# Projections in a deep Trainium2 kernel: one token tile after the other, or both in turns on each chunk of weights

## The chip, the core and the metric

The kernel runs on one core of one Trainium2 chip. The core has five engines that run side by side: TensorE (PE in the profile; PEld is its loading of the stationary operand), VectorE (DVE), ScalarE (ACT), GpSimd (POOL) and SyncE (SP), which here issues the DMA loads of all weights. Each engine takes its instructions in the order of its own queue, and an instruction that waits holds up everything behind it on that engine. The metric is the time of one execution in microseconds.

## What is computed

256 tokens of 1024 features go through nine sublayers, all in float32: two blocks of (FFN, mixer, FFN), where the first mixer is HGRN2 and the second is forgetting attention ("fox"), and a third block (FFN, token mixer, FFN) that is modulated by a vector c. The FFNs hold most of the products:

```python
def swiglu(h, w_in, w_out):                      # w_in 1024 x 5632, w_out 2816 x 1024
    gate, up = jnp.split(h @ w_in, 2, axis=-1)
    return (jax.nn.silu(gate) * up) @ w_out
...
proj = h @ w_in                                  # fox: q, k, v, g (1024 columns each), z_f
...
mod = (jax.nn.silu(c) @ w_ada[l] + b_ada[l]).reshape(b, N_SUB, 3, D_MODEL)   # third block
u = rms_norm(h, norm_pre[l, i]) * (1.0 + scale) + shift
h = h + resid_w * gate * rms_norm(fn(u), norm_post[l, i])
```

## The kernel before

**Products.** The tokens are two token tiles of 128 (t = 0 and 1). A sublayer's normalized input is transposed (L233) and split into a high part `uh` (a cast on ACT) and a rest `ul` (a subtraction on DVE), both by `split` (L166, L167). The activations are the stationary operand, and the weights stream through. Weights are split in the same way into `H` (ACT) and `L` (DVE), and each product is three passes (`mm3`): H by uh (L208), L by uh (L209), H by ul (L210).

**Weights.** They come in chunks of two k-tiles (2 x 128 rows) of 512 columns, 512 KB each. SP loads a chunk into one of five `raw` buffers (L177); the splits of a chunk free its buffer for the chunk five places on; `H` and `L` have six chunks each. A projection of 512 columns takes four chunks and eight k-tiles. `project` goes over them for one token tile: 8 k-tiles x 3 passes = 24 matmuls into one PSUM bank `acc` (five banks in that pool). The first projection to ask for a chunk loads it, the second token tile's 24 matmuls use the same tiles again.

**FFN** (`ffn`, L478). Its 2816 columns are cut into `SLICES`: five of 512 and one, the third, of 256. For each slice TensorE runs gate of t 0, the transposes of the slice before, gate of t 1, up of t 0, up of t 1. `gate` is a Silu on ACT, `up` a product on DVE. `out_stream` then adds up the product with `w_out` (22 k-tiles). A sublayer's first slice goes through `first_pair` (L387), which puts the second token tile's transposes behind the first products of t 0.

**Modulation beside it.** The third block's modulation is computed in jobs of 512 columns (`ada`, L844), spread over the sublayers 3, 5, 6, 7 and 8 (counted from 0; 4, 4, 4, 4 and 2 jobs). A job loads four chunks of `w_ada` through the same five `raw` buffers (L849) and a row of `b_ada`, and adds them up with two DVE operations a chunk (L851); its end is a split and two matmuls (L858). `side()` runs one step of a job; an FFN calls it after each projection of one token tile from the second slice on, four times a slice, and on in the out projection.

**Mixers.** `group(g)` makes two projections of both tiles by `pair` (L416) or, in the token mixer, by `values` and `both`. The small products of attention are tasks that `weave` puts between the pieces of projections by a planner's costs (`PACING`). In hgrn these are the decays (L612), scores (L636 to L645) and outputs (L660); in fox a head's scores (L783, L784), transposes (L793) and values (L802 to L804), with DVE's minimum (L787), ACT's exponential (L789), a DVE copy (L795) and a DVE product by the gate (L815) between them.

**Order.** TensorE's order is that in which the code is traced. Other engines' queues are ordered by a scheduler, in advance.

Of the kernel before, what the change touches and what calls it, by code (L numbers as in the profile page):

```python
"""Two pre-norm blocks of two layers (HGRN2 and forgetting attention as mixers), then a
modulated block with stick-breaking and differential attention, on 256 tokens.

Layout: the residual stream stays in SBUF as two tiles of 128 tokens. Every projection has
the activations (transposed, [feature, token]) as the stationary operand and streams the
weights. Both operands are split exactly into a part of float32r's 12 significant bits and
a rest, and hi*hi + hi*lo + lo*hi are summed in PSUM, so each product costs three
single-rate passes at float32's accuracy. The mixers' small products are plain float32.
"""
# [13 lines left out]
ALU = mybir.AluOpType  # L23
# [5 lines left out]
P = 128  # L29
# [4 lines left out]
CK = 2      # k-tiles of 512 columns in a chunk of weights  # L34
# how many tasks of a mixer are under way, the time between their starts and what else their chains take (see weave)
# [3 lines left out]
# (first column, columns) of the hidden slices of a feed-forward layer  # L39
SLICES = ((0, 512), (512, 512), (1024, 256), (1280, 512), (1792, 512), (2304, 512))  # L40

# columns of the array of constants
C_U = 0                 # [128, 9, 128] partial-sum columns: level 128 (first tile), 64..1, 128 (second tile)
C_LM = C_U + 9 * 128    # [128, 7, 64] which scores a level supplies
C_FOXM = C_LM + 7 * 64  # [128, 256] zeros | causal mask
C_SEL = C_FOXM + 256    # [128, 16] -1 in rows h and 32 + h of column h
C_DIST = C_SEL + 16     # [128, 384] -|t - s|, chunk-causal
C_STR = C_DIST + 384    # [128, 384] s < t
C_SUF = C_STR + 384     # [128, 128] -(j > s)
C_WIDE = C_SUF + 128    # [128, 128] the diagonal and the pairs of levels 64 and 32  # L50
# [3 lines left out]
def constants():  # L54
    """Arrays that depend on shapes alone."""
# [12 lines left out]
    c[:, C_FOXM + P:C_FOXM + 2 * P] = np.where(t <= s, 0.0, NEG)   # rows are queries here  # L68
# [3 lines left out]
    for k, (q0, k0) in enumerate(((0, 0), (P, 0), (P, P))):  # L72
        qp, kp = s + q0, t + k0                                    # rows are queries
        c[:, C_DIST + k * P:C_DIST + (k + 1) * P] = np.where(kp // 64 <= qp // 64, -np.abs(qp - kp), -1e34)
    for k, (k0, q0) in enumerate(((0, 0), (0, P), (P, P))):
        c[:, C_STR + k * P:C_STR + (k + 1) * P] = (s + k0) < (t + q0)   # rows are keys
# [5 lines left out]
class Program:  # L82
    """Traces the computation. The order of the tensor engine's instructions is that of this code (the
    other engines are left to the scheduler), so code that feeds it from slower chains is written as
    tasks (generators, see weave) that are woven into the streams of projections."""

    def __init__(self, tc, p, es):
# [36 lines left out]
        self.jobs = []      # generators that are run beside the projections, a step at a time  # L124

    def side(self):
        """A step of the jobs."""
# [41 lines left out]
    def loadw(self, views, shape, spare=False):  # L169
        """One chunk of weights, split: the views side by side in its last dimension. Returns (hi, lo) of its  # L170
        two halves (k-tiles, or columns of one k-tile). Spare chunks take tiles that stand idle at the ends
        of sublayers."""
# [243 lines left out]
    def pair(self, W1, W2, evac1, evac2, after1, after2, transposes=None):  # L416
# [4 lines left out]
        else:  # L421
            for t in range(NT):
                yield from self.project(t, W1, evac1)
# [801 lines left out]
```

## Time and profile before

| | |
|---|---|
| median of 3 runs | 1718.08 us (1717.99 to 1723.05) |
| span of the profiled execution | 1713.2 us (first to last instruction) |
| outside that span, against the median | 4.9 us |
| TensorE busy | 1667.1 us, 97% |
| VectorE busy | 1144.1 us, 67% |
| ScalarE busy | 911.8 us, 53% |
| GpSimd busy | 212.5 us, 12% |
| DMA | 328.45 MB, 192 GB/s on the mean |

One execution was profiled; its own device time was not listed apart, so the median of the three stands beside its span. Busy time of TensorE counts a matmul to its modelled end, which overlaps the next; the pitch from one start to the next is what a matmul costs. "Idle" in brackets is what an engine waited just before an instruction, with the engine and line that it waited for. PEclk is the granted clock, 1.00 at 2.4 GHz and near 0.5 at 1.2 GHz.

### The profile page before, as it was taken

Reading aid. Unit: us, or ns where it says so; the run is one execution under the profiler, and the core shown is the slowest. Engines: PE = TensorE matmul, PEld = TensorE weight load, DVE = VectorE, ACT = ScalarE, POOL = GpSimd, SP = SyncE. Lnnn points to the kernel's source line nnn. Section 1 sums busy time; section 2 is a strip of 40 time slices with the busy share of each in tenths; the row PEclk is TensorE's granted clock in tenths of the full one; section 3 lists DMA queues with packets and bytes.
Section 4 is the critical chain, followed back from the end, with each engine's and each line's share of the span. In section 5 each row is a group of like instructions: output and inputs, shape, how many; then the busy total and the mean of one; then the engine's idle time right before and its main releaser. Section 6 shows DMA issues by size and latency. Waiting matters only on the chain. (4 is left out here: it accounts for less than half of the span.)

```text
span 1713.2 us, 23351 instructions
## 1 busy us (share of the span) xinstructions
PE 1667.1 (97%) x8136; PEld 1386.2 (81%) x8136; DVE 1144.1 (67%) x2003; ACT 911.8 (53%) x1884; POOL 212.5 (12%) x275
## 2 busy tenths in 40 slices
PE   7999999999999999999999999999999999999998
PEld 5888888788888888888888878878887678778886
DVE  5555587776655677656566767578756678877663
ACT  5545466555544545546665544445545558564452
POOL 2000034330000010003120000110003321120000
PEclk9999999999999999999999999999999999999999
DMA  9555543325656588755345776568764456746652
GB/s 305 177 191 197 183 150 99 99 77 178 212 183 202 172 262 276 238 170 176 122 150 161 242 250 239 167 208 296 256 225 146 159 178 201 248 157 219 226 196 75
DMA packets 176886, 328.45 MB, mean 192 GB/s; under 512 B 12656, under 2 KB 65904, under 8 KB 176768
## 3 DMA queue, kind: packets, MB, share of 16 engines
q1 hardware_dynamic: 173328, 318.29, 56.4%
q0 software_dynamic: 3152, 8.15, 1.7%
q8 instruction: 64, 1.05, 0.2%
q14 instruction: 54, 0.44, 0.1%
q10 hardware_dynamic: 288, 0.52, 0.1%
HBM read 325.86 MB, written 1.05 MB: 191 GB/s over the span
## 5 line engine op out<-in xcount | busy, mean ns | idle before, releaser
L167 DVE TENSOR_TENSOR L<-raw,H 128x512 fp32r<-128x512 f32 (+1 forms) x1092 | 694.9, 681 | 221.6 <-ACT H L166 214.1
L166 ACT CAST H<-raw 128x512 fp32r<-128x512 f32 (+1 forms) x1092 | 599.4, 600 | 426.7 <-PE acc L210 301.8
L208 PE MATMUL acc<-H,uh 128*128 128x512 f32 (+1 forms) x1552 | 600.0, 387 | 1.3 <-ACT uh L166 1.3
L209 PE MATMUL acc<-L,uh 128*128 128x512 f32 (+1 forms) x1552 | 588.5, 379 | 5.9 <-DVE L L167 5.7
L210 PE MATMUL acc<-H,ul 128*128 128x512 f32 (+1 forms) x1552 | 587.0, 378 | 0.5 <-DVE ul L167 0.5
L209 PEld LDWEIGHTS acc<-L,uh 128*128 128x128 f32 x1552 | 294.1, 190 | 61.1 <-DVE L L167 12.0
L210 PEld LDWEIGHTS acc<-H,ul 128*128 128x128 f32 x1552 | 293.5, 189 | 55.5 <-DVE ul L167 1.4
L208 PEld LDWEIGHTS acc<-H,uh 128*128 128x128 f32 x1552 | 294.0, 189 | 52.7 <-ACT uh L166 1.9
L208 PE MATMUL acc<-H,w 128*128 128x512 f32 x536 | 209.8, 391 | 0.0
L209 PE MATMUL acc<-L,w 128*128 128x512 f32 x536 | 208.6, 389 | 0.0
L210 PE MATMUL acc<-H,q 128*128 128x512 f32 x512 | 199.4, 389 | 0.0
L851 DVE SCALAR_TENSOR_TENSOR ad<-raw,cs,ad 128x512 f32<-128x512 f32 x144 | 109.5, 761 | 93.5 <-DMA raw<-in_w_ada 78.6
L209 PEld LDWEIGHTS acc<-L,w 128*128 128x128 f32 x536 | 100.7, 188 | 20.6
L208 PEld LDWEIGHTS acc<-H,w 128*128 128x128 f32 x536 | 100.6, 188 | 20.5
L210 PEld LDWEIGHTS acc<-H,q 128*128 128x128 f32 x512 | 96.1, 188 | 20.1
L276 POOL TENSOR_SCALAR r<-s 128x1 f32<-128x1 f32 x24 | 15.9, 664 | 724.3 <-ACT o L259 482.3
L493 ACT ACTIVATE o<-acc 128x512 f32<-128x512 f32 (+1 forms) x72 | 40.4, 561 | 75.2 <-PE acc L210 75.1
L167 DVE TENSOR_TENSOR q<-T,w 128x512 fp32r<-128x512 f32 (+1 forms) x72 | 43.6, 639 | 45.6 <-ACT w L166 45.6
L233 PE MATMUL T<-ident,o 128*128 128x128 f32 x408 | 55.6, 276 | 14.5 <-DVE o L265 9.7
L498 DVE TENSOR_TENSOR o<-o,acc 128x512 f32<-128x512 f32 (+1 forms) x72 | 45.9, 637 | 34.9 <-PE acc L210 34.7
L233 PEld LDWEIGHTS T<-ident,o 128*128 128x128 f32 x408 | 47.7, 142 | 23.6 <-DVE o L265 9.7
L845 POOL MEMSET ad<- 128x512 f32 x18 | 9.5, 529 | 394.4 <-DVE ad L167 368.7
(244 smaller groups left out, 1440.6 us busy)
## 6 DMA issues: line engine op xcount, KB each, us to landing
raw<-in_ffn_w_in SPq DMA_DIRECT2D x160, 512.0 KB, 4.7
raw<-in_ffn_w_out SPq DMA_DIRECT2D x88, 512.0 KB, 4.2
raw<-in_w_ada SPq DMA_DIRECT2D x72, 512.0 KB, 5.2
raw<-in_ffn_w_down SPq DMA_DIRECT2D x44, 512.0 KB, 4.3
raw<-in_ffn_w_gate SPq DMA_DIRECT2D x40, 512.0 KB, 4.5
raw<-in_ffn_w_up SPq DMA_DIRECT2D x40, 512.0 KB, 4.5
raw<-in_hg_w_in SPq DMA_DIRECT2D x64, 256.0 KB, 3.2
raw<-in_fox_w_in SPq DMA_DIRECT2D x64, 256.0 KB, 3.6
```

The lines of the kernel that those rows point to most:

```text
L166: self.nc.scalar.copy(hi, src)
L167: self.nc.vector.tensor_sub(lo, src, hi.bitcast(F32))
L208: mm(out, xh, H, start=first, stop=False)
L209: mm(out, xh, L, start=False, stop=False)
L210: mm(out, xl, H, start=False, stop=last)
L233: self.nc.tensor.transpose(T[:, j, :], src[:, (k0 + j) * P:(k0 + j + 1) * P], self.ident)
L276: self.nc.gpsimd.tensor_scalar(r, s2[:, 0:1], s2[:, 1:2], EPS, op0=ALU.add, op1=ALU.add)
L493: self.last_silu = nc.scalar.activation(s[:, :n], A[:, :n], AF.Silu)
L498: nc.vector.tensor_tensor(s[:, :n], s[:, :n], A[:, :n], op=ALU.mult)
L845: nc.gpsimd.memset(a, 0.0)
L851: nc.vector.scalar_tensor_tensor(a, raw[:, k, :], self.cs[:, k0 + k:k0 + k + 1], a, op0=ALU.mult, op1=ALU.add)
```

## The change

A new generator, `project_both`, goes through a projection's four chunks and lets both token tiles use each chunk before the next. `pair` (in hgrn and fox), the token mixer's projections and the FFN's gates and ups use it; `first_pair` stays as it is. In the FFN's 256-column slice, gate's and up's columns are loaded side by side and make one product of 512 columns. `side()` still runs four steps in a slice of 512 columns, after every 8 of its 16 pieces of a projection, but two in that of 256. Comments are removed as well, which shifts line numbers: L166, L167 and L208 to L210 stay, L233 is L240 after, L265 is L272, L851 is L866, L793 is L808, L802 is L817.

```diff
+    def project_both(self, W, evac):
+        states = [{} for _ in range(NT)]
+        for k0 in range(0, 8, CK):
+            for t in range(NT):
+                yield from self.project(t, W, evac, k0, k0 + CK, states[t])
...
-            for t in range(NT):
-                yield from self.project(t, W1, evac1)
+            yield from self.project_both(W1, evac1)
             yield from after1
-            for t in range(NT):
-                yield from self.project(t, W2, evac2)
+            yield from self.project_both(W2, evac2)
         yield from after2
...
-            if c0:
-                self.side()
+
+        def run_both(W, evac, between=None):
+            for n, _ in enumerate(self.project_both(W, evac)):
+                if n == 7 and between is not None:
+                    transposes(*between)
+                if n % 8 == 7:
+                    self.side()
...
+            def gate_up(t, A):
+                gate(t, A)
+                up(t, A)
...
+            elif n == 256:
+                run_both(self.load_in([wgc, wuc], n), gate_up, before)
             else:
-                run(self.project(0, Wg, gate))
-                transposes(*before)
-                run(self.project(1, Wg, gate))
-                for t in range(NT):
-                    run(self.project(t, Wu, up))
+                run_both(self.load_in([wgc], n), gate, before)
+                run_both(self.load_in([wuc], n), up)
```

**TensorE in the second slice of the first FFN**, before: the end of `up` of the first token tile (bank acc_453) and the start of the second's (bank acc_511), which takes its weights from the start again.

```order
L208 MATMUL acc_453<-H_498,uh0_111 128x512
L209 MATMUL acc_453<-L_499,uh0_111 128x512
L210 MATMUL acc_453<-H_498,ul0_113 128x512
L208 MATMUL acc_511<-H_456,uh1_112 128x512
L209 MATMUL acc_511<-L_457,uh1_112 128x512
L210 MATMUL acc_511<-H_456,ul1_114 128x512
```

And the same projection now, from its second chunk (H_477) to the third (H_497):

```order
L208 MATMUL acc_453<-H_477,uh0_111 128x512
L209 MATMUL acc_453<-L_478,uh0_111 128x512
L210 MATMUL acc_453<-H_477,ul0_113 128x512
L208 MATMUL acc_468<-H_477,uh1_112 128x512
L209 MATMUL acc_468<-L_478,uh1_112 128x512
L210 MATMUL acc_468<-H_477,ul1_114 128x512
L208 MATMUL acc_468<-H_477,uh1_112 128x512
L209 MATMUL acc_468<-L_478,uh1_112 128x512
L210 MATMUL acc_468<-H_477,ul1_114 128x512
L208 MATMUL acc_453<-H_497,uh0_111 128x512
```

Each chunk now has 12 matmuls in a row, six for each tile; before, a chunk's two uses stood 24 matmuls apart, and the four chunks of a projection were first asked for within its first 24.

**VectorE at the start of sublayer 3**, the first with jobs, before. `o` are the halves of the normalized second token tile, `ul_114` the rest of its transposed halves, without which TensorE's passes L210 of that tile can't run, and `ad` is the sum of the first job.

```order
L265 SCALAR_TENSOR_TENSOR o_5229<-X_108,rs_5236,mod 128x512
L265 SCALAR_TENSOR_TENSOR o_5230<-X_108,rs_5236,mod 128x512
L167 TENSOR_TENSOR ul_114<-T,uh_112 128x512 x2
L167 TENSOR_TENSOR L<-raw,H 128x512 x8
L851 SCALAR_TENSOR_TENSOR ad<-raw,cs,ad 128x512
```

And the same place now:

```order
L272 SCALAR_TENSOR_TENSOR o_5073<-X_108,rs_5080,mod 128x512
L272 SCALAR_TENSOR_TENSOR o_5074<-X_108,rs_5080,mod 128x512
L866 SCALAR_TENSOR_TENSOR ad<-raw,cs,ad 128x512
L167 TENSOR_TENSOR ul_114<-T,uh_112 128x512 x2
L866 SCALAR_TENSOR_TENSOR ad<-raw,cs,ad 128x512
L167 TENSOR_TENSOR L<-raw,H 128x512 x8
```

The first step of a job has moved from behind eight weight splits to ahead of `ul_114`. On SP its load stands two chunks earlier too, in the eleventh place of the sublayer instead of the thirteenth. The starts of sublayers 5, 6, 7 and 8 show the same.

**TensorE at the end of fox**, before: the last head's values (L802 to L804), out products `acc<-H,o`, and the last transposes (L233).

```order
L802 MATMUL T<-q_8276,w_8417 128x64
L803 MATMUL T<-q_8276,w_8417 128x64
L804 MATMUL T<-q_8357,w_8417 128x64
L208 MATMUL acc<-H,o_6998 128x512
...
L210 MATMUL acc<-H,o_6999 128x512
L233 MATMUL T<-ident,w_8477 128x128 x2
L233 MATMUL T<-ident,w_8482 128x128 x2
```

And now, from the last out product that stands between the heads: transposes of head 2 (w_8146), scores of head 3 (L798, L799), values of head 2 (w_8242), transposes and values of head 3, the last transposes.

```order
L210 MATMUL acc<-H,o_6765 128x512
L808 MATMUL T<-ident,w_8146 128x128 x3
L798 MATMUL acc<-q_7771,q_8041 128x128
L799 MATMUL acc<-cT,sel 128x128
L798 MATMUL acc<-q_7771,q_8052 128x256
L799 MATMUL acc<-cT,sel 128x256
L817 MATMUL T<-q_8061,w_8242 128x64
L818 MATMUL T<-q_8061,w_8242 128x64
L819 MATMUL T<-q_8075,w_8242 128x64
L808 MATMUL T<-ident,w_8245 128x128 x3
L817 MATMUL T<-q_8061,w_8263 128x64
L818 MATMUL T<-q_8061,w_8263 128x64
```

Behind the last of these rows come L819 and then the four last transposes (L240) at once. Before, 12 out products stood between the last head's values and the last transposes, and six more between each pair of the head's steps; now the chain of the last head has no out products in it. Behind the last transposes stand 36 out products both times.

## Rows read from the trace of the kernel before

**Rows 1.** The page's busy times: us, share of the span, instructions of each engine.

```profile
PE 1667.1 (97%) x8136; PEld 1386.2 (81%) x8136; DVE 1144.1 (67%) x2003; ACT 911.8 (53%) x1884; POOL 212.5 (12%) x275
```

**Rows 2.** Stretches of sublayers 2 and 3: us, busy times, PEclk, DMA share, GB/s.

```profile
385.50:572.40 186.90, 186.90 (x902) 157.35 (x901) 107.01 (x177) 93.54 (x177) 2.38 (x4) 1.00 0.56 186
572.40:763.80 191.40, 189.70 (x910) 158.77 (x909) 131.06 (x218) 96.09 (x184) 11.77 (x22) 1.00 0.70 232
```

**Rows 3.** TensorE's waits over the span: total us, times, longest.

```profile
PE acc L209 <- DVE L L167: 5.7, 12, 1.2
PE T L977 <- POOL w L974: 3.9, 3, 1.8
PE T L643 <- DVE w L621: 3.7, 2, 3.3
```

**Rows 4.** TensorE's timeline in sublayer 0: start, us, instruction.

```profile
59.74 0.39 PE L208 MATMUL acc<-H,uh 128*128 128x512 f32 x1
...
61.55 0.39 PE L210 MATMUL acc<-H,ul 128*128 128x512 f32 x1
61.78 0.28 PE L208 MATMUL acc<-H,uh 128*128 128x256 f32 x1
...
64.41 0.28 PE L209 MATMUL acc<-L,uh 128*128 128x256 f32 x1
```

**Rows 5.** TensorE's timeline in sublayer 3, around its longest wait for weights.

```profile
629.19 0.28 PE L208 MATMUL acc<-H,uh 128*128 128x256 f32 x1
630.64 0.38 PE L209 MATMUL acc<-L,uh 128*128 128x256 f32 x1 [1.17 <-DVE L L167]
630.86 0.28 PE L210 MATMUL acc<-H,ul 128*128 128x256 f32 x1
```

**Rows 6.** VectorE's timeline at the same place.

```profile
626.06 2.33 DVE L851 SCALAR_TENSOR_TENSOR ad<-raw,cs,ad 128x512 f32<-128x512 f32 x3 [1.08 <-DMA raw<-in_w_ada]
...
630.17 1.42 DVE L167 TENSOR_TENSOR L<-raw,H 128x256 fp32r<-128x256 f32 x4
```

**Rows 7.** VectorE's waits in sublayer 5: total us, times, longest.

```profile
DVE ad L851 <- DMA raw<-in_w_ada: 19.0, 9, 2.9
DVE ad L851 <- DMA ad<-in_b_ada: 7.8, 2, 4.8
```

**Rows 8.** The load issued at 579.6, by DMA issues: KB, us to landing.

```profile
raw<-in_ffn_w_in SPq DMA_DIRECT2D x1, 512.0 KB, 4.7
```

**Rows 9.** VectorE's timeline at the starts of sublayers 3 and 5.

```profile
583.43 1.29 DVE L167 TENSOR_TENSOR ul<-T,uh 128x512 fp32r<-128x512 f32 x2 [1.56 <-ACT uh L166]
...
926.20 1.29 DVE L167 TENSOR_TENSOR ul<-T,uh 128x512 fp32r<-128x512 f32 x2 [1.60 <-ACT uh L166]
```

**Rows 10.** TensorE's timeline at the start of sublayer 3.

```profile
584.88 0.39 PE L210 MATMUL acc<-H,ul 128*128 128x512 f32 x1
```

**Rows 11.** TensorE's timeline at the end of fox.

```profile
901.93 0.33 PE L802 MATMUL T<-q,w 128*128 128x64 f32 x2
...
902.52 0.47 PE L208 MATMUL acc<-H,o 128*128 128x512 f32 x1
...
905.37 0.60 PE L233 MATMUL T<-ident,w 128*128 128x128 f32 x4
906.22 0.50 PE L208 MATMUL acc<-H,o 128*128 128x512 f32 x1 [0.24 <-ACT o L166]
```

**Rows 12.** VectorE's and ScalarE's timeline at the end of fox.

```profile
891.13 0.29 DVE L787 CUSTOM_DVE_ANT_0 w<-acc,mod 128x128 f32<-128x128 f32 x1 [0.20 <-PE acc L784]
...
892.58 0.50 ACT L789 ACTIVATE w<-w,nm 128x256 f32<-128x256 f32 x1
...
894.58 0.56 DVE L795 COPY w<-T 128x384 f32<-128x384 f32 x1 [0.64 <-PE T L793]
...
902.82 0.76 DVE L815 TENSOR_TENSOR w<-T,q 128x256 f32<-128x256 f32 x2 [2.85 <-PE T L804]
```

**Rows 13.** The stretch behind hgrn's longest wait, columns as in the second group.

```profile
313.00:319.00 6.00, 5.75 (x19) 4.94 (x20) 4.59 (x11) 1.06 (x3) 0.77 (x1) 0.58 0.44 162
```

More of the change, by code (lines that the diff above doesn't have):

```diff
@@ L497, in up @@
                 s = S[t, c0]
-                nc.vector.tensor_tensor(s[:, :n], s[:, :n], A[:, :n], op=ALU.mult)
-            Wg, Wu = self.load_in([wg[:, c0:c0 + n]], n), self.load_in([wu[:, c0:c0 + n]], n, 8 if before else self.spare())
+                nc.vector.tensor_tensor(s[:, :n], s[:, :n], A[:, 512 - n:512], op=ALU.mult)
+            def gate_up(t, A):
+                gate(t, A)
+                up(t, A)
+            wgc, wuc = wg[:, c0:c0 + n], wu[:, c0:c0 + n]
             if before is None:
-                run(self.first_pair(Wg, Wu, gate, up, self.pending))
-            else:
-                run(self.project(0, Wg, gate))
-                transposes(*before)
-                run(self.project(1, Wg, gate))
-                for t in range(NT):
-                    run(self.project(t, Wu, up))
+                run(self.first_pair(self.load_in([wgc], n), self.load_in([wuc], n, self.spare()), gate, up, self.pending))
+            elif n == 256:
+                run_both(self.load_in([wgc, wuc], n), gate_up, before)
+            else:
+                run_both(self.load_in([wgc], n), gate, before)
+                run_both(self.load_in([wuc], n), up)
             before = (c0, n)
@@ L918, in values @@
             if second is None:
-                for t in range(NT):
-                    yield from self.project(t, Wv, evac)
+                yield from self.project_both(Wv, evac)
             else:
@@ L936, in both @@
         def both(W, evac):
-            for t in range(NT):
-                yield from self.project(t, W, evac)
-                self.side()
+            for n, item in enumerate(self.project_both(W, evac)):
+                yield item
+                if n % 8 == 7:
+                    self.side()
         def turn(R, padded, scales):
```

## The prediction, made before the changed kernel was run

> **What bounds the kernel now.** The busy times come first: TensorE is busy for 97% of the span, the next engine, VectorE, for 67% [rows 1]. The profiled execution has a span of 1713.2 us; the median of the three runs is 1718.1, so 4.9 us lie outside the span, and I make the sum against the span and carry those 4.9 over. Next the stretches by sublayer: an FFN without jobs has no idle time on TensorE at all, one with four jobs takes 191.4 us instead of 186.9 and has 1.7 us of idle time [rows 2]. So the change can act in two ways only: by less work on TensorE, and by the few microseconds in which TensorE waits. The waits are listed next: 5.7 us in 12 waits of L209 for `L`, the weights' rest, and in the mixers 3.9 us in the token mixer and 3.7 us in hgrn [rows 3]. The reader should see that all removable waits together are under 2% of the time, so that this change is one of a few microseconds, in either direction. 0.3% of 1718.1 is 5.2 us, about what a measurement of this kernel can tell from no change.
>
> **The merged product.** A 512-column matmul starts 226 ns after the one before it (61.55 less 59.74, over 8 intervals), one of 256 columns 119.5 ns (64.41 less 61.78, over 22) [rows 4]. Six FFNs with 96 matmuls of 256 columns make 576 x 0.1195 = 68.8 us; in their place stand 288 of 512, 65.1 us. That is **-3.7 us**, all on TensorE in a stage without idle time, so all of it on the path. The Trainium skill, TensorE: Matmul & The Clock Gate, section "Back-to-back issue gap", gives N columns at 2.4 GHz plus 2.5 ns as the gap, 109 and 216 ns; by it the merge would save 0.7 us, an estimate from that page. The trace disagrees by 10 ns for both sizes, and the trace's pitch is taken.
>
> **Waits for L in the FFNs.** The longest is at 630.64: TensorE's L209 comes 1.45 us after the matmul before it, and the next another 0.22 after that, where both pitches should be 0.12 [rows 5]. So a wait of 1.17 us costs 1.43, that is its length and 0.26. Twelve cost 5.7 + 12 x 0.26 = 8.8 us. What VectorE did before: it waited 1.08 us for a `w_ada` load, ran three job steps, and only then came to the splits [rows 6]. In sublayer 5 such waits are 19.0 us in nine for `w_ada` and 7.8 us in two for `b_ada`, the longest 2.9 and 4.8 [rows 7]. A job step that waits for its data holds up the weight splits behind it, and TensorE runs out of split chunks. Before, a projection needs four new chunks in its first 24 matmuls (5.4 us) and none in the next 24; five `raw` buffers and six split chunks give a lead that is spent in the first half: four chunks ahead last 5.4 us. Now it needs one each 12 matmuls (2.7 us), so four chunks ahead last 10.8 us, more than the longest of those waits and four splits behind it. I take **-8.0 us**, a wait or two being left; the bounds are 0 (the waits return elsewhere) and -8.8.
>
> **The job step ahead of `ul`.** This is the price that the order shows. At the start of sublayer 3 VectorE waited 1.56 us for the cast `uh` and then ran the two `ul` from 583.43, 0.65 us each [rows 9]; TensorE used the first at 584.88 [rows 10]. Now a job step stands between the norm and `ul`, and its load has the eleventh place on SP. The load that had this place before was issued at 579.6 and landed 4.7 us later, at 584.3 [rows 8]. A step takes 0.78 us (2.33 for three [rows 6]), so the first `ul` ends at 584.3 + 0.78 + 0.65 = 585.7 instead of 584.1, and TensorE waits 0.8 us and 0.26 to restart: 1.1 us. Nothing covers it, since the passes behind L210 in TensorE's queue belong to the same product. Sublayer 5 starts in the same way (`ul` at 926.20 after a wait of 1.60 [rows 9]), and sublayer 6 is taken alike: 3.3 us for the three. In 7 and 8 the second tile's transposes come later in `first_pair` (behind six more matmuls), so that the load can be there in time; 0 to 1.1 each, I take 0.3 as nearer to nothing. Together **+4.0 us**; bounds 0 (the loads land before the cast ends) and, with the longest `w_ada` wait of 2.9 us [rows 7] instead of 0.8 at all five, 5 x 3.2 = +16.
>
> **The end of fox.** Before, out products stand between all steps of the last heads; the last head's values (901.93) are 2.85 us ahead of the last transposes (902.52 to 905.37), which hides VectorE's product L815 (0.76 us from 902.82), and the one wait left is 0.24 [rows 11, 12]. Now the last head's steps follow each other bare. From its scores to its transposes stand a wait of 0.20, two minima (0.29 for the smaller) and an exponential of 0.50 [rows 12], some 1.5 us, against which head 2's values run, 0.59 (901.93 to 902.52 [rows 11]): 0.9 us. From transposes to values a copy of 0.56 [rows 12] and its handover, 0.8. From values to the last transposes 0.30 and up to 0.76, 0.9. That is 2.6 us. Whether the clock falls is open: behind hgrn's wait of 3.3 us TensorE had a granted clock of 0.58 for 6 us [rows 13], 1.2 GHz for most of it, a loss of 2.5 us; the three waits here are shorter and have short matmuls between them. I take half, 1.3, between 0 and 2.5. Sum **+3.9 us**, bounds +2.6 and +5.1; less than 2.6 only if the scheduler's cover on VectorE were idle, which the bare order excludes.
>
> **hgrn, the token mixer, the rest.** In hgrn both tiles' evacuations now follow each other by 6 matmuls, so units start later in the stream, and the last unit's transposes stand directly before the out products that need them: +0.8, as for fox's copy above. In the middle fewer weight splits stand ahead of L621 on VectorE, for which the 3.3 us were waited; I take two, of 0.65 like a `ul` [rows 9], -1.3. I take **-0.5 us**; bounds: the long wait and its half clock (3.3 + 2.5 [rows 3, 13]) gone, or there once more, so -6 to +6. In the token mixer TensorE's order hardly moves: 0, bounds one wait for L974's work more or less (3.9 us [rows 3]). In the third slice 16 weight splits become 8 of twice the width on ACT and DVE, engines that are busy 53% and 67% [rows 1], and two job steps less fall into it and go on into the out projection: 0, at most a wait for a step of 0.78 in each of four such sublayers. Banks: a projection holds two of five over its length and gives them up 6 matmuls apart; the next needs two more, and the out projection its third and fourth only 12 matmuls later: 0, at most 0.6 us (a product `up`) at six ends.
>
> **Sum.** -3.7 - 8.0 + 4.0 + 3.9 - 0.5 = -4.3: span 1708.9, time **1713.8 us**, say 1714.
>
> **Rivals.**
> *More is hidden than I charge.* The `w_ada` loads land before the cast (their place on SP was reached early, SP waits for buffers, not for data), -4.0; or hgrn's long wait goes with its half clock, -5.3 beyond what I took. One gives 1708.5 to 1710, both 1704. For it: the lead in chunks is longer everywhere. Against: 579.6 + 4.7 is later than the norm.
> *The FFN waits stay.* They come from late job data, and VectorE still waits in its queue for them, with the weight splits behind it. Then -8.0 falls away: 1721.8, no change that can be measured. For it: 19.0 us of such waits in one sublayer. Against: the lead of 10.8 us above.
> *Slower: the job step ahead of `ul`.* If the five loads come late by 2.9 us, as the longest wait in sublayer 5, instead of 0.8, each start costs 3.2 and the sum rises by 12: 1725.8. It decides from where each start costs 2.7 us: 13.4 instead of 4.0, 1723.2. For it: DMA share 0.70 in sublayer 3 [rows 2], and at a sublayer's start several loads queue. Against: the load in the same place took 4.7 us.
> *The merge saves nothing.* Twice 119.5 less 226 is 13 ns, and the gain rests on these. If they belong to that stretch and not to the number of matmuls, 288 pairs save 0: 1717.5. Against: both pitches are means over many intervals in one stretch. The formula of the Trainium skill's page above (TensorE: Matmul & The Clock Gate, "Back-to-back issue gap") comes near this rival: 1716.8 by it, an estimate.
>
> **How the numbers follow.** My sum 0.42 (1710 to 1717.5), more hidden 0.22, FFN waits stay 0.16, slower 0.16, merge for nothing 0.04. Faster than 1712.9: nearly all of the second and somewhat under half of the first, 0.38. Slower than 1723.2: most of the fourth and a little of the third, 0.17. The rest, 0.45, is within. The range 1704 to 1724 leaves out about 0.08 below and 0.12 above.
>
> **What would show it.** The page should have 512-column products in all FFNs, 3.7 us less TensorE work, and the wait of L209 for `L` (5.7 us) below 1 us. A new wait of L210 for `ul`, about 0.8 us, should stand at the starts of sublayers 3, 5 and 6. At the end of fox three waits of 0.8 to 0.9 us (for ACT or DVE: exponential, copy, L830) should stand. hgrn should still have a wait of L658 for w from L636. I am wrong if L209's waits keep more than half of their length, if the starts cost nothing or over 2.7 us each, or if hgrn's stretch moves by more than 3 us.

## The result and the profile after

The changed kernel takes 1727.74 us (median of 5 runs, 1723.73 to 1729.98) where the kernel before takes 1717.99 (5 runs beside it): the ratio is 1.0051, with a 95% interval of 1.0034 to 1.0068. It is slower, and outside the range that was given. The profiled execution has a span of 1726.6 us; single executions of one kernel differ by several us here, so the 13.4 us between the two spans are read as places, and the sizes are taken from repeated runs where it matters. In the runs from here on 1.7 to 2.9 us lie outside the span (1.85 here), not the 4.9 that the prediction carried over; by that, an estimate, the profiled execution of the kernel before took some 1715 us, about 3 less than its median, and so much of the 13.4 is not the change's.

The page's busy times of the changed kernel: TensorE has as much to do as before [rows 1]; the 3.7 us less that were forecast don't show in this total, since its busy time in fox alone rises by 5.3 us, as the rows of fox below show.

```profile
PE 1668.2 (97%) x7848; PEld 1368.4 (79%) x7848; DVE 1140.6 (66%) x1955; ACT 910.9 (53%) x1836; POOL 205.7 (12%) x275
```

The stretches of sublayers 2 to 4 and 6 after, from one first cast of `uh` to the next (us, busy times of PE, PEld, DVE, ACT and POOL, PEclk, DMA share, GB/s):

```profile
382.20:568.90 186.70, 186.66 (x855) 154.80 (x854) 105.51 (x167) 92.86 (x170) 2.52 (x4) 1.00 0.60 182
568.90:760.00 191.10, 189.18 (x862) 156.06 (x861) 129.43 (x210) 96.40 (x177) 11.79 (x22) 1.00 0.71 232
760.00:918.90 158.90, 156.12 (x834) 129.86 (x833) 98.12 (x228) 96.30 (x241) 31.37 (x50) 0.98 0.47 141
...
1113.00:1309.80 196.80, 190.60 (x860) 155.47 (x859) 132.77 (x213) 97.19 (x180) 16.29 (x21) 1.00 0.69 225
```

Sublayer 4, fox, before:

```profile
763.80:915.20 151.40, 150.79 (x835) 128.17 (x834) 96.54 (x229) 95.77 (x242) 34.24 (x50) 1.00 0.49 148
```

All nine stretches, in us:

| sublayer | 0 FFN | 1 hgrn | 2 FFN | 3 FFN, jobs | 4 fox | 5 FFN, jobs | 6 FFN, jobs | 7 token mixer, jobs | 8 FFN, jobs |
|---|---|---|---|---|---|---|---|---|---|
| before | 188.3 | 185.1 | 186.9 | 191.4 | 151.4 | 194.2 | 192.9 | 209.6 | 201.3 |
| after | 187.7 | 183.1 | 186.7 | 191.1 | 158.9 | 194.1 | 196.8 | 214.5 | 202.3 |

The reader sees three things. An FFN without jobs gains a little. The FFNs with jobs gain nothing in two and lose in two, although the change was made in them above all. Fox loses 7.5 us and the token mixer 4.9.

TensorE's waits after (total, times, longest):

```profile
PE T L240 <- DVE o L509: 9.3, 10, 1.9
...
PE acc L210 <- DVE ul L167: 4.9, 4, 1.6
PE T L992 <- POOL w L989: 4.0, 2, 3.6
...
PE acc L209 <- DVE L L167: 0.7, 1, 0.7
```

The wait for weight splits went from 5.7 us to 0.7 [rows 3]. In its place stand two that were hardly there: the transposes (L240) wait for the `up` product (L509), 9.3 us in ten, and the passes L210 for `ul`, 4.9 us in four (one of them, 1.0 us, in the first sublayer, which has no job). The same two before:

```profile
PE T L233 <- DVE o L498: 0.6, 1, 0.6
PE acc L210 <- DVE ul L167: 0.5, 1, 0.5
```

**The wait for ul** stands where the prediction put it. VectorE at the start of sublayer 3 after, and TensorE at the same place:

```profile
576.92 1.42 DVE L272 SCALAR_TENSOR_TENSOR o<-X,rs,mod 128x512 f32<-128x512 f32 x2 [0.84 <-POOL rs L285]
581.19 0.75 DVE L866 SCALAR_TENSOR_TENSOR ad<-raw,cs,ad 128x512 f32<-128x512 f32 x1 [2.86 <-DMA raw<-in_w_ada]
581.86 1.28 DVE L167 TENSOR_TENSOR ul<-T,uh 128x512 fp32r<-128x512 f32 x2
```

```profile
581.12 0.39 PE L209 MATMUL acc<-L,uh 128*128 128x512 f32 x1
582.60 0.50 PE L210 MATMUL acc<-H,ul 128*128 128x512 f32 x1 [1.10 <-DVE ul L167]
```

VectorE waits 2.86 us for the job's load with `ul` behind it, and TensorE comes 1.25 us late (1.48 between the two starts instead of 0.23).

**The wait for the up product** is the same thing at another place. VectorE in sublayer 5 after, and TensorE there:

```profile
1008.92 1.54 DVE L866 SCALAR_TENSOR_TENSOR ad<-raw,cs,ad 128x512 f32<-128x512 f32 x2 [2.15 <-DMA raw<-in_w_ada]
1010.38 1.29 DVE L167 TENSOR_TENSOR L<-raw,H 128x512 fp32r<-128x512 f32 x2
1011.58 1.28 DVE L509 TENSOR_TENSOR o<-o,acc 128x512 f32<-128x512 f32 x2
```

```profile
1010.00 0.39 PE L210 MATMUL acc<-H,ul 128*128 128x512 f32 x1
1012.32 0.92 PE L240 MATMUL T<-ident,o 128*128 128x128 f32 x5 [1.93 <-DVE o L509]
```

A job step waits for its load, two splits follow, and the two `up` products, both of them now, since the tiles end six matmuls apart, come behind.

**Fox's end** after: TensorE, and the granted clock of two stretches (PEclk; columns as above):

```profile
901.92 0.47 PE L799 MATMUL acc<-cT,sel 128*128 128x256 f32 x1
902.22 0.36 PE L817 MATMUL T<-q,w 128*128 128x64 f32 x2
...
903.30 0.33 PE L808 MATMUL T<-ident,w 128*128 128x128 f32 x1 [0.27 <-ACT w L804]
903.80 0.44 PE L808 MATMUL T<-ident,w 128*128 128x128 f32 x2 [0.17 <-ACT w L804]
904.88 0.43 PE L817 MATMUL T<-q,w 128*128 128x64 f32 x2 [0.65 <-DVE w L810]
...
906.35 1.11 PE L240 MATMUL T<-ident,w 128*128 128x128 f32 x4 [0.59 <-DVE w L830]
907.50 0.79 PE L208 MATMUL acc<-H,o 128*128 128x512 f32 x1
...
912.78 0.41 PE L208 MATMUL acc<-H,o 128*128 128x512 f32 x1
```

```profile
902.00:907.50 5.50, 3.79 (x22) 2.51 (x21) 2.42 (x11) 1.36 (x5) 3.83 (x7) 0.86 0.38 102
907.50:913.50 6.00, 6.00 (x16) 4.70 (x17) 2.48 (x8) 1.10 (x3) 0.13 (x1) 0.56 0.53 18
```

In the bare chain TensorE is idle for 1.7 of 5.5 us, in four waits; then 12 out products take 5.28 us (907.50 to 912.78) where at 226 ns they take 2.71, so the half clock costs 2.6 us. Before, the same place had one wait of 0.24 [rows 11], and fox ran at the full clock (1.00 in its row above).

### The profile page after: what moved, and what is told of

Same layout as the page of the kernel before. It is cut to its first block, busy times and chain, and to the rows that moved or that the text cites. A ratio compares the mean times of both kernels' runs of the same rounds, so it can differ in the third digit from the quotient of the medians.

```text
span 1726.6 us, 22637 instructions
## 1 busy us (share of the span) xinstructions
PE 1668.2 (97%) x7848; PEld 1368.4 (79%) x7848; DVE 1140.6 (66%) x1955; ACT 910.9 (53%) x1836; POOL 205.7 (12%) x275
## 5 line engine op out<-in xcount | busy, mean ns | idle before, releaser
L167 DVE TENSOR_TENSOR L<-raw,H 128x512 fp32r<-128x512 f32 x1044 | 694.0, 707 | 307.3 <-ACT H L166 301.5
L166 ACT CAST H<-raw 128x512 fp32r<-128x512 f32 x1044 | 594.0, 619 | 528.9 <-PE acc L210 406.9
L208 PE MATMUL acc<-H,uh 128*128 128x512 f32 x1456 | 581.1, 399 | 1.5 <-ACT uh L166 1.4
L210 PE MATMUL acc<-H,ul 128*128 128x512 f32 x1456 | 569.6, 391 | 4.9 <-DVE ul L167 4.9
L209 PE MATMUL acc<-L,uh 128*128 128x512 f32 x1456 | 568.9, 391 | 0.7 <-DVE L L167 0.7
L210 PEld LDWEIGHTS acc<-H,ul 128*128 128x128 f32 x1456 | 274.1, 188 | 65.1 <-DVE ul L167 7.1
L208 PEld LDWEIGHTS acc<-H,uh 128*128 128x128 f32 x1456 | 274.8, 189 | 56.5 <-ACT uh L166 2.0
L209 PEld LDWEIGHTS acc<-L,uh 128*128 128x128 f32 x1456 | 274.8, 189 | 54.1 <-DVE L L167 1.2
L208 PE MATMUL acc<-H,w 128*128 128x512 f32 x536 | 209.7, 391 | 0.0
L209 PE MATMUL acc<-L,w 128*128 128x512 f32 x536 | 208.6, 389 | 0.0
L210 PE MATMUL acc<-H,q 128*128 128x512 f32 x512 | 199.3, 389 | 0.0
L866 DVE SCALAR_TENSOR_TENSOR ad<-raw,cs,ad 128x512 f32<-128x512 f32 x144 | 108.9, 756 | 132.9 <-DMA raw<-in_w_ada 105.1
L208 PEld LDWEIGHTS acc<-H,w 128*128 128x128 f32 x536 | 100.6, 188 | 20.5
L209 PEld LDWEIGHTS acc<-L,w 128*128 128x128 f32 x536 | 100.7, 188 | 20.4
L210 PEld LDWEIGHTS acc<-H,q 128*128 128x128 f32 x512 | 96.1, 188 | 20.0
L240 PE MATMUL T<-ident,o 128*128 128x128 f32 x408 | 59.0, 282 | 22.5 <-DVE o L509 9.3
L240 PEld LDWEIGHTS T<-ident,o 128*128 128x128 f32 x408 | 47.2, 143 | 37.7 <-DVE o L509 14.3
L632 POOL TENSOR_TENSOR w<-w,w 128x512 f32<-128x512 f32 (+1 forms) x32 | 44.6, 1412 | 40.0 <-ACT w L630 40.0
L509 DVE TENSOR_TENSOR o<-o,acc 128x512 f32<-128x512 f32 (+1 forms) x72 | 44.6, 635 | 4.7 <-PE acc L210 3.0
```

The costliest lines, as they stand in the source:

```text
L166: self.nc.scalar.copy(hi, src)
L167: self.nc.vector.tensor_sub(lo, src, hi.bitcast(F32))
L208: mm(out, xh, H, start=first, stop=False)
L209: mm(out, xh, L, start=False, stop=False)
L210: mm(out, xl, H, start=False, stop=last)
L240: self.nc.tensor.transpose(T[:, j, :], src[:, (k0 + j) * P:(k0 + j + 1) * P], self.ident)
```

## The experiments

**Which part loses.** Two kernels with one half of the change each. The first takes `pair` and the token mixer's two places from the kernel before, the second the whole of `ffn`.

```diff
-            yield from self.project_both(W1, evac1)
+            for t in range(NT):
+                yield from self.project(t, W1, evac1)
             yield from after1
-            yield from self.project_both(W2, evac2)
+            for t in range(NT):
+                yield from self.project(t, W2, evac2)
```

> The FFNs as in the changed kernel, the mixers' projections one token tile after the other as before. Theory (most of the loss is in fox and the token mixer, and the FFNs give back what they gain): the sublayers 1, 4 and 7 return to 185, 151 and 210 us, the six FFNs keep +2.9 us over before (the sum of their stretches in the trace of the changed kernel), so about 1721 (1718 to 1724). Rival (the FFNs gain what was predicted, 3.7 + 8.0 less 3.7, and all of the loss is the mixers'): about 1710.

> The mixers' projections in turns, the FFNs as before. Theory: fox +7.5 and the token mixer +4.9 as in the changed kernel's stretches, hgrn -2.0, together about 1728 (1726 to 1731), slower than before. Rival (the token mixer's loss comes with the FFNs' job steps ahead of it, not with its own order): fox and hgrn alone, +5.5, about 1723.5; by the prediction's terms it would be 1721.4.

The FFNs alone: 1717.2 us, ratio 0.9994 (0.9979 to 1.001), no change that can be told, and between the two expectations (the six stretches in the table above add up to +3.7, not +2.9). The mixers alone: 1728.2, ratio 1.0057 (1.0037 to 1.0077), the theory's time. Its stretches make up for some 7 us of that: fox 157.8 us (+6.4), the token mixer 211.9 (+2.3), hgrn 183.4 (-1.7). The rest stands in FFNs with unchanged code, sublayers 2, 3, 5 and 6, each 0.8 to 1.3 us longer than in the trace before, and what of it is the change's is open. So the mixers' part carries the whole loss, and the FFNs' part, which should have gained 8 to 12 us, gives all of it back.

**The merged product by itself**: the kernel before, with gate and up of the third slice in one product.

```diff
+            if n == 256:
+                W = self.load_in([wg[:, c0:c0 + n], wu[:, c0:c0 + n]], n)
+                run(self.project(0, W, gate_up))
+                transposes(*before)
+                run(self.project(1, W, gate_up))
```

> The kernel before with the third slice's gate and up in one product and nothing else; two job steps less fall into that slice. By the matmuls' starts in sublayer 2 after (11.6 us of 256-column matmuls gone, 11.1 of 512 more) 0.5 us in each of six FFNs: 1715.0. By the prediction's term 1714.3; by the isolated gap 1717.3. A rival: the waits for L grow, as a chunk is used up by 6 matmuls where it has 12 of half size, no difference there: 0 more.

1713.8, ratio 0.9981 (0.9964 to 0.9998): 3.3 us less, with 0.3 to 6.2 in the interval. The stretch of sublayer 2 is 186.3 us instead of 186.9 in this run, as in most with the merge; six times that is 3.6. Sublayer 0 moves alike: 187.7 or 187.8 us in 14 of the 15 executions with the merge, 188.4 in both without it. That fits the prediction's term of 3.7; the interval holds as well the 0.7 us that the prediction estimates from the isolated gap of the Trainium skill (TensorE: Matmul & The Clock Gate, "Back-to-back issue gap"), the stretches do not.

**The loads' lateness.** The changed kernel, whose job steps read a still tile instead of the loaded weights:

```diff
-                nc.vector.scalar_tensor_tensor(a, raw[:, k, :], self.cs[...], a, ...)
+                nc.vector.scalar_tensor_tensor(a3, self.still[:, None, :].to_broadcast([P, n // 256, 256]), self.cs[...], a3, ...)
```

> The changed kernel with the same loads for the jobs, but its job steps read a tile that lies still in SBUF instead of the loaded weights, so that they never wait for a load (the modulation is then not the reference's). Theory (late job data in front of other work on VectorE makes the new waits): the waits for ul at three FFN starts (4.4 us with their restarts), for the up product (9.3 and ten restarts, 11) and part of the token mixer's (the 3.6 us one and its half clock) go: 1707 (1703 to 1713). Rival (VectorE has too much work in these places, with or without data): at most a third goes, 1722 or more.

1712.2, ratio 0.9961 (0.9947 to 0.9976): 15 us less than the changed kernel against the same kernel before, inside the theory's range, at its upper end. The waits for the up product and for `ul` at the three starts are gone, and sublayers 3 and 5 take 188.2 us each, against 191.1 and 194.1. The scheduler also moved the steps, so this shows that late job data cost that much, not yet by which queue.

**Fox's end.** The changed kernel, but fox's last group of heads takes its projections one tile after the other:

```diff
+            take = self.project_both if both else self.project_each
...
-    ..., self.pending if g == 0 else None)
+    ..., self.pending if g == 0 else None, both=g < 3)
```

> The changed kernel, but in fox's last group of heads alone the two projections take one token tile after the other, as before; this gives the last head's steps six out products between them again. Theory (fox loses at its end, by the bare chain and the half clock behind it): fox's stretch goes from 158.9 to 151 to 153 us, the time to about 1720.5. Rival (the turns delay the heads in every group): fox stays above 156, the time above 1725.

1722.1, ratio 1.0029 (1.0015 to 1.0044). Its stretch of fox:

```profile
758.40:911.20 152.80, 151.88 (x835) 127.90 (x833) 97.63 (x229) 96.20 (x241) 31.66 (x50) 1.00 0.49 146
```

152.8 us at the full clock. Two groups still take turns (the first goes through `first_pair` in every kernel), and 6 of the 7.5 us are gone with the last group's order. The theory holds for the stretch; the time is 3.8 us less than the changed kernel's by the ratios, 5.7 by the medians. Fox's loss is in its last group.

**The first step behind ul again.** On the kernel with the FFNs alone, the first call for a job step in each FFN is left out:

```diff
                 if n % 8 == 7:
-                    self.side()
+                    if skip[0]:
+                        skip[0] -= 1
+                    else:
+                        self.side()
```

> The run with only the FFNs changed, and in each FFN the first of its calls for a job step is left out (the jobs go on a step later), so that the first job load stands in the thirteenth place of the sublayer again and the step behind ul. Theory: the waits of L210 for ul go from 3.9 us in three (the first FFN's 1 us may stay) to at most 1.2, with their restarts -3.9, about 1713.5. Rival (what is late comes later, and the waits for the up product grow by as much): 1717.

1713.5, ratio 0.9963 (0.9946 to 0.9979), the theory's time. Of the waits for `ul` only the first FFN's 1.0 us is left. Those for the up product are 9.1 us in eight, though, against 7.3 in eight in the run with the FFNs alone, and sublayers 3, 5 and 6, whose starts had waited, take 582.2 us together, as they did there (582.0). So what these starts gained was lost again in the same stretches, in part to the waits that the rival named, and where the 3.7 us of the time came from is not shown.

**Later transposes**, on the run before:

```diff
-                if n == 7 and between is not None:
+                if n == 11 and between is not None:
```

> The run before this one, and the transposes of the slice before stand after 36 of the next gate's 48 matmuls instead of 24, 2.7 us later. Theory (the up product waits behind job steps on VectorE, by up to 2.3 us): the waits for the up product, 7.3 us in eight and their restarts, 9 in all, go down to under 1.5 us: about 1706. Rival (a late job load holds up whatever is next in VectorE's queue, the weight splits again): the waits of L209 for L come back with 4 us or more, 1711 or above.

1717.5, ratio 0.9986 (0.9968 to 1.0003): the theory's 1706 was missed. TensorE's waits of this run show what came:

```profile
PE T L240 <- DVE o L515: 6.8, 6, 1.8
PE acc L208 <- DVE o L515: 5.7, 2, 3.9
```

The up product is so late that first the transposes and then the next product's bank, which it still holds, wait for it. The rival that named the weight splits was wrong as well (L209 waits 0.7 us). Moving the one who waits does not help; the product must come earlier.

**Turns in hgrn** in addition. The edit is against the changed kernel: with the FFNs and the token mixer as in the run before, it takes fox alone back to one tile after the other, and hgrn keeps its turns.

```diff
-            yield from self.pair(Wqk, Wvg, qk, vg, tasks, ...)
+            yield from self.pair(Wqk, Wvg, qk, vg, tasks, ..., both=False)
```

> The FFNs of the run before this one, and turns in hgrn, whose stretch was 1.6 and 2.0 us shorter with them in the two runs that had them; fox and the token mixer as before. Theory: 1.5 us less than the run before it, about 1704.5, 13 to 14 us less than the kernel before. Rival: the hgrn difference is that of two executions, not of the order: 1706, or as the run before it.

1718.4, ratio 1.0 (0.9985 to 1.0016): nothing gained over the run before it; the rival holds. hgrn's stretch is 184.5 us here with turns and 180.7 in the run with the first step left out, which has none: it varies between executions by more than the order could have given.

**Loading a step ahead**, on two kernels:

```diff
+        following = load(0)
+        yield 1
         for k0 in range(0, 8, CK):
-            raw = self.rawp.tile(...)
-            nc.sync.dma_start(raw, p["w_ada_2"][...])
+            raw, following = following, load(k0 + CK) if k0 + CK < 8 else None
```

> The run with the FFNs changed and the first step left out (1713.5), and each job loads its next chunk of w_ada one step before it is added up, b_ada's row too, so that a load has 24 more matmuls (5.4 us) to land; the order of steps and products on VectorE's queue stays alike. Theory (VectorE waits for late job loads with the up product behind): VectorE's waits for w_ada and b_ada fall to under a third, TensorE's waits for the up product from 9.1 us in eight to under 3, time about 1705.5 (1703 to 1709). Rival (a job now holds one of the five weight buffers for longer, and the weights come late): waits of L209 for L of 4 us or more, 1711 or above.

> The same edit of the jobs on the kernel with the merged product alone (1713.8), where each tile still takes its projection whole. Theory: the waits of L209 for L, 8.9 us in seven and their restarts, 10.7 together, fall to under 3: about 1705; then the turns have no part in the gain. Rival: with four chunks asked for in 24 matmuls the longer hold of a buffer costs more here than with turns: 1711 or above, and the turns would be worth 5 us or more with loads issued ahead.

1712.3 (0.9961, 0.9947 to 0.9976) and 1712.8 (0.9963, 0.995 to 0.9976): neither theory's time came. VectorE's waits for the jobs' loads in the first of the two:

```profile
DVE ad L878 <- DMA raw<-in_w_ada: 96.8, 53, 5.6
...
DVE ad L878 <- DMA ad<-in_b_ada: 15.9, 5, 4.2
```

They are no shorter than without the edit (98.2 and 15.6), and the traces show why: the edit changed nothing that ran. In both pairs every engine has the same instructions in the same order with the edit and without it, the loads on SP included, and from a load's issue to its step pass 4.9 us on the mean in the first pair, with or without (5.4 and 5.5 in the second, where the waits for `L` stay too, 9.3 us in eight). In the code a step comes one call later than its load; the scheduler put it where it had been. So these runs say nothing of earlier loads or of the buffers. They are repeats: the merged product alone measures 6.4 us less in the second (4.1 to 8.6) where it measured 3.3.

**The place in VectorE's queue.** Each job step is queued behind the latest `up` product:

```diff
-                nc.vector.tensor_tensor(s[:, :n], s[:, :n], A[:, 512 - n:512], op=ALU.mult)
+                self.last_up = nc.vector.tensor_tensor(s[:, :n], s[:, :n], A[:, 512 - n:512], op=ALU.mult)
...
+                with self.tc.issue_after(self.last_up.ins) if self.last_up is not None else contextlib.nullcontext():
-                nc.vector.scalar_tensor_tensor(a, raw[:, k, :], ...)
+                    nc.vector.scalar_tensor_tensor(a, raw[:, k, :], ...)
```

> The run with the FFNs changed and the first step left out (1713.5), and each job step is queued on VectorE behind the latest up product, so that a step that waits for its load can't stand in front of it. Theory (the place in VectorE's queue, not the amount of work or the load's time, makes TensorE wait): the waits for the up product, 9.1 us in eight and their restarts, fall to under 2, about 1704 (1701 to 1708). Rival (whatever is next in the queue waits, the weight splits): waits of L209 for L of 4 us or more take their place, 1711 or above.

> The same, and the jobs load a step ahead as well. Theory: with the step's place fixed, the earlier load now does shorten VectorE's waits for w_ada (from 97 us to under 60), and TensorE's waits for the up product and for L are under 2 us together: 1703, 0 to 2 us below the run before it. Rival (TensorE doesn't wait any more, so it's worth nothing, or the buffer held longer costs): the same as the run before it or up to 3 us more.

> The changed kernel as it is, mixers too, with that queueing alone (no step left out, loads as they were). Theory: in the FFNs the waits for the up product (9.3 us, ten, 11 with restarts) and for ul (three, 4.4, as the first step of a sublayer can no longer stand ahead of the first up products, and so not ahead of ul) go; fox and the token mixer keep their +7.5 and +3 to 5: 1727.7 - 15.4, about 1712. Rival: less than half of that, 1720 or above.

> The kernel with the merged product alone (1713.8), each tile's projection whole, with that queueing. Theory (with the whole projection of one tile, four chunks are asked for in 24 matmuls, and a late step holds up weight splits, which the queueing doesn't change): waits of L209 for L stay near 8.9 us, 1713; the turns are then worth the 9 us between this run and the first of the four. Rival (the turns are worth nothing once the steps stand behind the up products): within 3 us of that first run.

On the changed kernel itself: 1712.5, ratio 0.996 (0.9944 to 0.9976), the theory's 1712. VectorE's waits for `w_ada`, and TensorE's for the up product (L509 is L510 here, L208 is L209):

```profile
DVE ad L868 <- DMA raw<-in_w_ada: 17.4, 12, 4.5
```

```profile
PE acc L209 <- DVE o L510: 1.6, 2, 1.1
```

In the changed kernel the same line is

```profile
DVE ad L866 <- DMA raw<-in_w_ada: 105.1, 54, 5.1
```

TensorE, SP and GpSimd have the same order in both kernels; only VectorE's and ScalarE's differ. So VectorE's waits for the same loads, in the same buffers, fall from 105.1 us to 17.4 by order alone: a step now comes 14.0 us after its load's issue on the mean instead of 4.8. The waits for the up product become 1.6 us, none of the three starts waits for `ul`. With the first step left out besides: 1712.0 (0.9963, 0.9946 to 0.998), not the 1704 expected. This run has a wait that the theory did not have:

```profile
PE acc L209 <- DVE o L516: 9.9, 3, 4.6
```

Those are banks again. With loads ahead as well it is far slower, 1745.2 (1.0156, 1.0135 to 1.0176). Again the loads keep their places on SP; what moved are the steps, 18.6 us behind their loads' issue instead of 14.9, so that a `raw` buffer is held for longer. TensorE has such waits (10.7 us in three), others for the up product (5.5) and for the jobs' ends by ACT and VectorE (8.9); together they are 15 us more than without the edit, less than half of the loss, and the rest was not settled. Without turns, on the merge alone: 1710.6 (0.9949, 0.993 to 0.9967). The theory expected waits for `L` of 9 us there; they are 0.3, so turns are not needed against these. The time is the rival's, within 3 us of the run with turns and the first step left out; but that run has the 9.9 us for banks in it, and the next experiment shows what the turns are worth without them.

**Both losses taken away**: the changed FFNs with the steps queued, the mixers as before.

> The changed FFNs with the job steps queued behind the latest up product, and the mixers' projections one token tile after the other as before. Theory (the two losses add up: the queue's in the FFNs, the order's in fox and the token mixer): 1712.5 of the run with the mixers in turns, less 7 in fox and 2 to 4 in the token mixer, about 1703 (1701 to 1706), below both kernels. Rival (with the steps queued the mixers' loss is hidden or comes back elsewhere, as in the run that also left the first step out, 1712.0): 1709 or above.

1703.75 (1697.52 to 1705.68), where the kernel before took 1723.2 beside it: ratio 0.9894 (0.9878 to 0.9911), faster than both kernels and than every other run. Sublayer 5 in it:

```profile
905.60:1093.80 188.20, 188.20 (x862) 156.27 (x861) 130.76 (x207) 94.06 (x174) 10.12 (x14) 1.00 0.72 231
```

TensorE has no idle time in this FFN with four jobs, nor in sublayer 3 (188.2 us too); sublayer 6 still takes 192.0. The two losses add up as the theory had it. The run that also left out the first step (1712.0) differs from this one in that step alone; its waits for banks, 9.9 us in three, are 1.2 us in one here.

It also settles the turns. This run and the one on the merge alone have the same queueing and the same mixers, and differ in the FFNs' turns: 0.9894 (0.9878 to 0.9911) against 0.9949 (0.993 to 0.9967), each against the kernel before beside it. So with the steps queued the turns in the FFNs are worth 9 us by the ratios, 7 by the medians, and the rival of that run falls. In place of waits for `L`, TensorE without turns waits for the jobs' ends (their two matmuls, L871 there):

```profile
PE T L871 <- ACT ad L167: 3.5, 3, 1.6
...
PE T L871 <- DVE ad L168: 3.0, 3, 1.4
```

All six are in sublayers 3, 5 and 6, which take 578.3 us together without turns and 568.4 with them, where no such wait is left. Why the turns take these waits away was not tested.

## Why the prediction was wrong, step by step

**Waits for L in the FFNs, -8.0: the step that failed.** Its first half was right, these waits went from 5.7 us to 0.7. But the step asked only how long the split chunks last while VectorE waits for a job's load, and not what else stands behind that wait in VectorE's queue. The bound of 0 for "the waits return elsewhere" was named and given little weight, and the one term that had the `up` product in it, under banks, was put at 0, at most 0.6 us at six ends. They did return: 9.3 us before the transposes, ten restarts besides (0.26 us each, as the prediction measured them), since a projection's two `up` products now come together at its end and job steps stand ahead of them. The run with the queueing shows it: with the steps behind `up` and TensorE's and SP's orders unchanged, 15 us come back. The rival "the FFN waits stay", 0.16, had nearly the right size and the wrong place. Nor was the longer lead in chunks needed: with the steps queued the waits for `L` are gone without turns as well. The 7 to 9 us that the turns are worth then are close to the term's 8.0 by luck, as they come from the jobs' ends.

**The job step ahead of ul, +4.0 (its parts add up to 3.9): right as a wait.** Three starts, 1.25, 1.36 and 1.78 us late by the starts of the matmuls, 4.4 in all against 3.3 for these three; sublayers 7 and 8, for which 0.6 was taken, wait nothing. Leaving out one step removed these waits, but the three stretches took as long, so that run does not show them as a price of their own.

**The end of fox, +3.9: the mechanism right, the size wrong.** 7.5 us in the trace after, 6.4 in the run with the mixers alone; fox takes 157.6 to 158.9 us in the four executions with turns in it and 151.2 to 151.4 in the twelve without. The idle time in the chain was 1.7 us in four waits, not 2.6 in three. The half clock cost 2.6 where 1.3 was taken: the bound of 2.5 taken from hgrn's long wait was the right value, though no wait here was longer than 0.65. What is left, some 3 us, may be small matmuls and transposes at the lower clock (four transposes in 1.11 us, 0.60 before [rows 11]), restarts, and waits earlier in fox such as 0.50 us at 801.78; it is not divided further, and stays open.

**The token mixer, 0: too low, and the stretch not settled.** 214.5 us against 209.6. In the trace VectorE waits 2.23 us for `w_ada` with the chain's products behind it, GpSimd's product comes late, and TensorE waits 3.59 us:

```profile
1357.04 0.75 DVE L866 SCALAR_TENSOR_TENSOR ad<-raw,cs,ad 128x512 f32<-128x512 f32 x1 [2.23 <-DMA raw<-in_w_ada]
1357.71 0.55 DVE L550 SCALAR_TENSOR_TENSOR w<-acc,w 128x384 f32<-128x384 f32 x1
...
1360.03 0.99 POOL L989 TENSOR_TENSOR w<-w,mod 128x384 f32<-128x384 f32 x1 [5.04 <-DVE w L988]
1362.18 1.32 POOL L989 TENSOR_TENSOR w<-w,mod 128x384 f32<-128x384 f32 x1 [1.16 <-DVE w L988]
```

```profile
1361.07 1.65 PE L992 MATMUL T<-w,mod 128*128 128x384 f32 x2 [3.59 <-POOL w L989]
```

It is the late job data again: with the still tile there is no such wait. Behind the latest `up` product the steps of a mixer are not held back, and in the run with that queueing all 17.4 us of VectorE's waits for `w_ada` lie in the token mixer, and TensorE's wait for GpSimd stays (3.45 us). But the stretch with the still tile is 212.7 us all the same, so this wait is not the whole of the loss. Five executions with the new order took 211.9 to 214.5 us, twelve with the old one 209.6 to 216.5. Some 2 us on the mean, but the two overlap.

**hgrn, -0.5**: -2.0 in this trace; over the runs no difference can be told, though in each of the six traces with turns in it the wait of 3.3 us is down to 1.1. **The merge, -3.7**: measured 3.3 with a wide interval and 6.4 in the repeat, 3.6 by sublayer 2's stretch; right in size as far as this goes. In the trace after, sublayer 2 gained just 0.2.

**Sum.** Merge -3.6 or so, `L` -7.8 (5.0 us and eleven restarts) and up product +11, `ul` +4.4, fox +7, token mixer +2: +13, against a measured 9.8 and the 13.4 between the two traces, from which most of these terms are read. The measured time less the up product's 11 us and fox's other 3 is the forecast's, 1713.7; that it fits so well is partly luck, since the token mixer's 2 us were forecast as nothing.

## What to carry to other kernels

When a queue is held up by an operation that waits for a load, removing the engine that visibly suffers moves the wait to whatever stands next in that queue: list all that stands behind it and who waits for each, before counting a gain. Where a scheduler orders queues in advance, fix the place of background steps behind the work that the bounding engine needs; here that was worth 15 us on the changed kernel, and only then did the FFNs' turns gain anything, 7 to 9 us. Read from the trace that an edit moved what it was meant to move before drawing on its time: loading a step ahead moved no load at all. When a stream of products is also the cover of a dependent chain, look at the end of the stream in the order of instructions: what was filler between the last steps is gone once the planner starts them later.

## What was not expected of the hardware

Four waits of 0.17 to 0.65 us among small matmuls were followed by 5.3 us at 1.2 GHz (a granted clock of 0.56 over 6 us), while the full clock held through a wait of 1.93 us in sublayer 5, between full products (PEclk 1.00 around it):

```profile
1009.00:1012.00 3.00, 1.38 (x7) 0.81 (x5) 2.96 (x5) 0.83 (x2) 0.00 (x0) 1.00 0.84 294
1012.00:1015.00 3.00, 2.69 (x15) 2.23 (x16) 2.01 (x4) 2.42 (x5) 0.00 (x0) 1.00 0.90 295
```

The loss, 2.6 us, was as large as the 2.5 behind hgrn's single wait of 3.3 us [rows 3, 13].
